# First norms of a four-FFN trunk: order of the opening loads, zero products while TensorE waits, operand parts taken from the PSUM banks

## The chip, the cores and the metric

One core of one Trainium2 chip runs the whole program. The metric is the device time of one execution in microseconds (us); for the kernel before it is the median of 3 executions. Engines are called as the profile calls them: PE (TensorE matmul), PEld (its weight load), DVE (VectorE), ACT (ScalarE), POOL (GpSimd), SP (SyncE, which here only issues DMAs). A "q" behind a name is the engine's sequencer, the place where DMAs are issued.

## The reference, cut to what matters

Two token batches, 512 and 256 rows of 1024 floats, go through the same trunk: layer 0 (a gated linear recurrence between two FFNs) and layer 1 (windowed attention between two FFNs), then a last norm. What the change touches is the very first step, the norm in front of the first FFN, and the first products of that FFN:

```python
def rmsnorm(x, g):
    xf = x.astype(F32)
    y = xf * lax.rsqrt(jnp.mean(xf * xf, axis=-1, keepdims=True) + NORM_EPS)
    return (y * g.astype(F32)).astype(x.dtype)

def swiglu_ffn(x, w1, w2):
    gate, up = jnp.split(x @ w1, 2, axis=-1)
    return (jax.nn.silu(gate) * up) @ w2

for li in range(DEPTH):
    x = x + 0.5 * swiglu_ffn(rmsnorm(x, norm_g[li, 0]), ffn_w1[li, 0], ffn_w2[li, 0])
    ...
```

All inputs are float32, `w1` is 1024 x 5632 and `w2` is 2816 x 1024 in each of the four FFNs.

## The kernel before, in words

**Tiling.** The 768 rows are six blocks of 128 rows (`x[0]` to `x[5]`), one tile of 128 x 1024 each, and two halves of three blocks. A norm (`norm_block`, L301) makes one block: ACT squares it and sums along the row (L304), ACT takes the root (L305), DVE the reciprocal (L306), and DVE multiplies the block by it (L307) into a tile `xn`. `turn` (L311) then transposes one half: for each of the eight 128-column pieces m it makes three PE transposes into one PSUM bank (L324), and ACT moves the bank out with the norm's weight as a factor (L327). `part` 0 is m = 0 to 3, `part` 1 is m = 4 to 7.

**Products.** A float32 product is made of three: every operand is split into a high part `hi` (rounded to fp32r by ACT) and a low part `lo` (DVE: value minus `hi`), and `mm3` (L260) adds hi·hi, hi·lo and lo·hi. L262, L263 and L264 are these three. For the transposed x the split is `put` and `split` (L267 on ACT, L268 on DVE), on two pieces at a time; for the weights `plain_steps` (L170 on ACT, L171 on DVE). The first two column tiles of an FFN are made in this plain form by `up_plain`, for each half of the rows a gate product (c = 0) and an up product (c = 1), each 8 pieces x 3 matmuls of 128x384. The others use a Strassen-like form with seven products, whose operands are sums and differences of the quarters of x, made by `sums`/`mix` (L351 to L355), and of w (L204, L217, POOL's `into`, L145).

**Order.** The program is traced in the order of the Python code. A planner in the compiler then orders the instructions of each engine: of those that its own cost model holds to be ready, the one traced first goes first, and a buffer must be free. `issue_after(i)` puts what is traced inside it behind `i` in the queue of `i`'s engine; it adds no wait for `i` to finish. An engine works through its queue strictly in order. `later` and `run_later` keep a list of steps that are traced at fixed places inside `up_plain` (L408) and elsewhere.

**Start.** `setup` (L92) loads the identity on SP (L101) and the norm weights as rows on ACT's queue (L109), transposes these rows on PE (L112) and copies them out on DVE (L114). `load_x` (L270) loads x[0] to x[2] on SP, then the first two weight tiles (L155), then x[3] to x[5]; norms blocks 0 to 2; turns half 0; stages (splits) the two weight tiles; and calls `load_tables` (L116), one small DMA on ACT's queue and one POOL instruction. The norms of blocks 3 to 5, the turns of half 1 and `sums` are put on the list for later. `down_quad` (L465) of the first group begins with additions in place among the six x blocks (L471, L472); their sources are ready as soon as x is loaded.

**Buffers.** PSUM has 8 banks under one tag, `big` tiles 21 slots, raw weights 4 (`wr`), split weights 8 (`w`).

## Time and profile before

| what | value |
|---|---|
| median of 3 executions | 2763.64 us (2762.39 to 2764.43) |
| profiled execution, its own time | 2764.33 us |
| span of the profiled execution, first to last instruction | 2762.5 us |
| mean granted TensorE clock over the span | 0.999 |
| PE busy | 2735.5 us in 17281 matmuls |
| DVE, ACT, POOL busy | 2102.6, 1326.6, 309.4 us |

How to read it: the profile is one execution, with the start and length of every instruction. The page gives totals; the timeline gives single instructions in order of time (start, length, engine, line, operation, tiles, count, and in brackets how long the engine sat idle before and what ended that); the windows view gives the busy time of each engine in a stretch, the granted clock (PEclk) and the DMA rate; the groups view gives sums by line and shape. Matmuls are pipelined, so the length of one is longer than the distance to the next: for throughput the distance counts.

### The profile page before, as it was taken

How to read it: one execution, taken by the hardware profiler on the slowest of the kernel's cores; microseconds unless marked ns; L12 is line 12 of the kernel's file. 1: busy time of each engine (PE TensorE's matmuls, PEld its weight loads, DVE VectorE, ACT ScalarE, POOL GpSimd, SP SyncE). 2: the span in 40 equal slices, each digit the busy share in tenths (PEclk: the TensorE clock that was granted, in tenths of full speed). 3: DMA queues.
4: the chain of work that ended last, by engine and by line, in shares of the span. 5: the costliest groups of instructions: out<-in, count | busy, mean ns of one | idle time of the engine just before them, and what ended most of it. 6: DMA issues, size and time to landing. Idle time of an engine off the chain costs nothing.

```text
span 2762.5 us, 44483 instructions
## 1 busy us (share of the span) xinstructions
PE 2735.5 (99%) x17281; PEld 2481.5 (90%) x17281; DVE 2102.6 (76%) x3662; ACT 1326.6 (48%) x2479; POOL 309.4 (11%) x315
## 2 busy tenths in 40 slices
PE   8999999999999999999999999999999999999998
PEld 8999999888888889999999999999886789999997
DVE  7888788557477568777888878887846768788877
ACT  7444444456466354443446444444546654443444
POOL 1111211000000001121111112111000001221111
PEclk9999999999999999999999999999999999999999
DMA  5544554321110324465444355544512123555443
GB/s 160 135 117 116 138 134 119 118 67 40 55 47 25 122 62 114 112 143 133 118 120 109 83 131 138 133 115 115 146 53 77 47 62 81 134 137 128 120 112 107
DMA packets 330116, 291.63 MB, mean 106 GB/s; under 512 B 11608, under 2 KB 257840, under 8 KB 329904
## 3 DMA queue, kind: packets, MB, share of 16 engines
q1 hardware_dynamic: 294064, 212.43, 25.8%
q0 software_dynamic: 31680, 62.93, 13.4%
q10 hardware_dynamic: 4160, 13.42, 1.4%
q8 instruction: 135, 2.21, 0.3%
q14 instruction: 77, 0.63, 0.1%
HBM read 216.39 MB, written 9.44 MB: 82 GB/s over the span
## 4 chain that ended last, share of the span: by engine, by line
PE 85%; DVE 10%; ACT 3%; issue 2%; DMA 0%; DVEq 0%; ACTq 0%; SPq 0%
PE ps L422 32%; PE ps L486 21%; PE ps L262 9%; PE ps L263 9%; PE ps L264 9%; DVE w L204 2%; DVE big L268 2%; PE ps L682 1%; PE ps L1218 1%; PE ps L1157 1%; PE ps L827 1%; PE ps L1209 1%; ACT w L203 1%; DVE wr L217 1%; PE ps L324 1%
## 5 line engine op out<-in xcount | busy, mean ns | idle before, releaser
L422 PE MATMUL ps<-big,w 128*128 128x384 f32 x6720 | 1174.6, 335 | 3.4 <-ACT tA L439 2.7
L422 PEld LDWEIGHTS ps<-big,w 128*128 128x128 f32 x6720 | 1165.4, 188 | 10.9 <-ACT tA L439 9.1
L203 ACT CAST w<-wr 128x512 fp32r<-128x512 f32 x600 | 415.3, 707 | 699.8 <-DVE wr L217 376.3
L204 DVE TENSOR_TENSOR w<-wr,w 128x512 fp32r<-128x512 f32 (+1 forms) x520 | 452.8, 874 | 180.1 <-ACT w L203 153.9
L486 PE MATMUL ps<-w,big 128*128 128x512 f32 x2520 | 575.9, 389 | 1.2 <-DVE x L508 1.2
L486 PEld LDWEIGHTS ps<-w,big 128*128 128x128 f32 x2520 | 472.4, 188 | 99.6 <-ACT big L267 1.6
L508 DVE SCALAR_TENSOR_TENSOR x<-ps,x 128x512 f32<-128x512 f32 x468 | 303.5, 680 | 10.5 <-PE ps L264 10.0
L145 POOL DMA_DIRECT2D s<-wr x120 | 105.0, 875 | 1667.5 <-DMA wr<-in_ffn_w_dram 784.5
L262 PE MATMUL ps<-w,big 128*128 128x512 f32 x624 | 252.5, 405 | 0.3
L264 PE MATMUL ps<-w,big 128*128 128x512 f32 x624 | 244.6, 392 | 0.9 <-DVE big L331 0.9
L263 PE MATMUL ps<-w,big 128*128 128x512 f32 x624 | 244.4, 392 | 0.0
L262 PE MATMUL ps<-big,w 128*128 128x384 f32 (+2 forms) x640 | 219.2, 344 | 2.1 <-ACT big L267 1.3
L267 ACT CAST big<-tA 128x384 fp32r<-128x384 f32 x296 | 148.0, 513 | 149.3 <-DVE tA L454 69.0
L263 PE MATMUL ps<-big,w 128*128 128x384 f32 (+2 forms) x640 | 216.4, 338 | 0.9 <-DVE big L268 0.6
L264 PE MATMUL ps<-big,w 128*128 128x384 f32 (+2 forms) x640 | 215.6, 337 | 0.0
L268 DVE TENSOR_TENSOR big<-tA,big 128x384 fp32r<-128x384 f32 x296 | 183.0, 629 | 12.7 <-ACT big L267 11.6
L171 DVE TENSOR_TENSOR w<-wr,w 128x1024 fp32r<-128x1024 f32 x92 | 111.8, 1221 | 79.0 <-ACT w L170 73.1
L262 PEld LDWEIGHTS ps<-w,big 128*128 128x128 f32 x624 | 117.2, 188 | 29.3 <-issue 6.0
L170 ACT CAST w<-wr 128x1024 fp32r<-128x1024 f32 x92 | 96.5, 1052 | 97.8 <-PE ps L263 77.8
L204 POOL TENSOR_TENSOR w<-wr,w 128x512 fp32r<-128x512 f32 x80 | 123.3, 1541 | 177.5 <-ACT w L203 156.4
L264 PEld LDWEIGHTS ps<-w,big 128*128 128x128 f32 x624 | 117.1, 188 | 27.6 <-DVE big L331 1.7
L263 PEld LDWEIGHTS ps<-w,big 128*128 128x128 f32 x624 | 117.4, 188 | 21.8 <-issue 0.4
(163 smaller groups left out, 2899.6 us busy)
## 6 DMA issues: line engine op xcount, KB each, us to landing
wr<-in_ffn_w_dram SPq DMA_DIRECT2D x264, 512.0 KB, 3.9
s<-in_ffn_w_dram SPq DMA_DIRECT2D x120, 256.0 KB, 3.3
s<-wr POOLq DMA_DIRECT2D x120, 256.0 KB, 4.5
wr<-wr POOLq DMA_DIRECT2D x80, 256.0 KB, 3.7
wr<-in_hg_w_in_dram SPq DMA_DIRECT2D x40, 512.0 KB, 3.8
wr<-wr POOLq DMA_DIRECT2D x20, 512.0 KB, 4.6
spill<-x ACTq DMA_DIRECT2D x12, 512.0 KB, 2.7
x<-spill ACTq DMA_DIRECT2D x12, 512.0 KB, 3.3
```

The costliest lines, as they stand in the source:

```text
L145: self.nc.gpsimd.dma_start(out, src, accum_op=ALU.add)
L171: self.nc.vector.tensor_sub(lo, raw, hi.bitcast(F32))
L203: nc.scalar.copy(h, src)
L204: low = (eng or nc.vector).tensor_sub(l, src, h.bitcast(F32)).ins
L262: nc.tensor.matmul(out, a[0], b[0], start=first, stop=False)
L263: nc.tensor.matmul(out, a[0], b[1], start=False, stop=False)
L264: nc.tensor.matmul(out, a[1], b[0], start=False, stop=last)
L267: self.nc.scalar.copy(hi, src)
L268: self.nc.vector.tensor_sub(lo, src, hi.bitcast(F32))
L422: self.nc.tensor.matmul(ps, a[x], b[y], start=first and k == 0 and i == 0, stop=k == 3 and i == 2, skip_group_check=True,)
L486: nc.tensor.matmul(ps, a[x], w[y], start=name == chain and kp == 0 and q == 0, stop=kp == 1 and q == 2, skip_group_check=True,)
L508: self.nc.vector.scalar_tensor_tensor(x, ps, c, x, ALU.mult, ALU.add)
```

## The change

The change rewrites the opening. The diff, cut to what the text speaks of:

```diff
+WARM = 21
...
     def setup(self, consts):
+        zero = self.tmp(TA)[:, :P]
+        nc.vector.memset(zero, 0.0)
         self.eps = cp.tile([P, 1], F32, name="eps")
         nc.vector.memset(self.eps, EPS)
+        idle = self.ps(P)
+        for _ in range(WARM):
+            nc.tensor.matmul(idle, zero, zero, start=True, stop=True)
+        raw = self.tmp(P)
+        nc.scalar.dma_start(raw, ident)
         warm = self.stat(1)
         nc.scalar.activation(warm, self.eps, AF.Sqrt)
-        raw = self.tmp(P)
-        nc.sync.dma_start(raw, ident)
...
-        pt = self.ps(n)
-        nc.tensor.transpose(pt, cols[:n, :], self.ident[:n, :n])
         self.cols = cp.tile([P, n], F32, name="cols")
-        nc.vector.tensor_copy(self.cols, pt)
+        def turn():
+            pt = self.ps(n)
+            nc.tensor.transpose(pt, cols[:n, :], self.ident[:n, :n])
+            nc.vector.tensor_copy(self.cols, pt)
+        self.turn_cols = turn
...
     def load_x(self, srcs):
...
-                order = self.norm_block(b)
-        self.turn(0, 0, 0)
-        self.turn(0, 1, 0)
+                order = self.norm_block(b, b == 1)
+        with self.tc.issue_after(self.scaled):
+            self.turn_cols()
+        self.turn(0, 0, 0, True)
         with self.tc.issue_after(order):
             self.stage_next()
             self.stage_next()
-        self.load_tables()
-        def rest():
-            for b in range(HB, NBLK):
-                self.norm_block(b)
-        self.later(rest, lambda: self.turn(1, 0, 0), lambda: self.turn(1, 1, 0), self.sums)
+        self.turn(0, 1, 0, True)
+        for b in range(HB, NBLK):
+            with self.tc.issue_after(order):
+                order = self.norm_block(b)
+        self.normed, self.mixed = order, self.scaled
+        with self.tc.issue_after(order):
+            self.load_tables()
+        self.later(lambda: None, lambda: None, lambda: self.turn(1, 0, 0), lambda: self.turn(1, 1, 0), self.sums)
 
-    def norm_block(self, b):
+    def norm_block(self, b, on_dve=False):
...
+        if on_dve:
+            nc.vector.tensor_tensor_reduce(xn, self.x[b], self.x[b], 1.0, 0.0, ALU.mult, ALU.add, r)
+        else:
+            nc.scalar.activation(xn, self.x[b], AF.Square, accum_out=r)
...
-        nc.vector.tensor_scalar(xn, self.x[b], r, None, ALU.mult)
+        self.scaled = nc.vector.tensor_scalar(xn, self.x[b], r, None, ALU.mult).ins
...
     def turn(self, half, part, row, straight=False):
...
+            if straight:
+                key = (f"b{part}{half}", m % 4 // 2)
+                if key not in self.ops:
+                    self.ops[key] = self.big([P, 2, 2, H], F32R)
+                hi, lo = (self.ops[key][:, m % 2, i, :] for i in range(2))
+            elif feeds_ffn:
                 nc.scalar.activation(self.block(part, half, m % 4), pt, AF.Copy, scale=g)
                 continue
...
             nc.scalar.activation(hi, pt, AF.Copy, scale=g)
             nc.vector.scalar_tensor_tensor(lo, pt, g, hi.bitcast(F32), ALU.mult, ALU.subtract)
...
+            if straight:
+                self.block(part, half, 0)
+                hi, lo = (self.ops[(name, kp)][:, :, i, :].bitcast(F32) for i in range(2))
+                nc.gpsimd.tensor_add(self.tn[(part, half)][:, kp], hi, lo)
+            else:
+                low = self.put(name, kp, self.tn[(part, half)][:, kp])
+                self.mixed = self.mixed and low
...
     def up_plain(self, tag, j, half):
-        self.nc.scalar.activation(t, pss[0], AF.Silu)
+        with self.tc.issue_after(self.normed) if self.normed else nullcontext():
+            self.nc.scalar.activation(t, pss[0], AF.Silu)
+        self.normed = None
...
     def down_quad(self, tag, g, hid):
-                nc.vector.tensor_add(x12, x12, x22)
-                nc.vector.tensor_sub(x21, x21, x22)
+                with self.tc.issue_after(self.mixed) if self.mixed else nullcontext():
+                    nc.vector.tensor_add(x12, x12, x22)
+                    nc.vector.tensor_sub(x21, x21, x22)
+            self.mixed = None
```

In words: the identity is loaded on ACT's queue, so that x is first on SP. PE multiplies a tile of zeros by itself 21 times before its first real work. The square of block 1 is made by DVE instead of ACT. The transposed norm weights are copied out by DVE behind the scaling of block 2. For half 0, ACT writes the high parts straight from the banks, DVE makes the low parts straight from the banks, and the sum of the two, which `sums` needs as the whole value, is made by POOL (four additions of 128x768). The norms of blocks 3 to 5 are traced in `load_x`; the first Silu, the small table of sinks, and the additions in place of the first `down_quad` are queued behind them (the additions behind the last split of half 1).

More of the change, by code (lines that the diff above doesn't have):

```diff
@@ L342, in put @@
         t = self.ops[(name, kp)] = self.big([P, 2, 2, H], F32R)
-        self.split(src, t[:, :, 0, :], t[:, :, 1, :])
+        return self.split(src, t[:, :, 0, :], t[:, :, 1, :])
     def operand(self, name, k):
```

15 lines of the change are left out of this document (7 added, 8 removed).

## Prediction

> **What bounds the kernel now.** I read the page's totals and the chain that ended last first, then the windows view of the opening.
>
> ```profile
> PE 2735.5 (99%) x17281; PEld 2481.5 (90%) x17281; DVE 2102.6 (76%) x3662; ACT 1326.6 (48%) x2479; POOL 309.4 (11%) x315
> PE 85%; DVE 10%; ACT 3%; issue 2%; DMA 0%; DVEq 0%; ACTq 0%; SPq 0%
> 30.00:60.00 30.00, 30.00 (x178) 29.97 (x177) 27.90 (x37) 20.44 (x35) 3.65 (x3) 1.00 0.30 80
> 13.64:17.05 3.41, 1.71 (x8) 1.46 (x9) 2.47 (x4) 3.41 (x7) 0.00 (x0) 1.00 1.09 338
> 17.05:20.47 3.42, 3.27 (x11) 2.77 (x10) 3.10 (x5) 3.42 (x5) 0.00 (x0) 0.50 1.17 290
> ```
>
> PE carries the span; 27 of 2762.5 us are free of it. From 30 us on it never pauses for 30 us (third row), so a gain of the opening is kept if nothing else becomes late, and it cannot exceed what PE loses before 30 us. The last two rows (after the window: PE, PEld, DVE, ACT, POOL busy, then granted clock) show one of these losses: 3.41 us at half clock, behind a stretch of the same length in which PE was half busy. The others stand in the timeline:
>
> ```profile
> 0.74 0.39 SPq L101 DMA_DIRECT2D tB<-in_ident_dram  x1
> 1.18 1.37 SPq L278 DMA_DIRECT2D x<-in_x_prompt_dram  x3
> 5.58 1.06 ACT L304 ACTIVATE big<-x 128x1024 f32<-128x1024 f32 x1 [2.89 <-DMA x<-in_x_prompt_dram]
> 7.23 0.38 PE L112 MATMUL ps<-ident_r,tB 88*128 88x88 f32 x1 [7.23 <-DMA tB<-in_hg_g_norm_dram]
> 6.96 1.04 ACT L304 ACTIVATE big<-x 128x1024 f32<-128x1024 f32 x1
> 8.33 1.04 ACT L304 ACTIVATE big<-x 128x1024 f32<-128x1024 f32 x1
> 10.02 0.75 DVE L307 TENSOR_SCALAR big<-x,stat 128x1024 f32<-128x1024 f32 x1
> 10.07 1.05 ACT L170 CAST w<-wr 128x1024 fp32r<-128x1024 f32 x1 [0.28 <-DMA wr<-in_ffn_w_dram]
> 11.16 1.22 DVE L171 TENSOR_TENSOR w<-wr,w 128x1024 fp32r<-128x1024 f32 x1 [0.38 <-ACT w L170]
> 8.09 5.38 PE L324 MATMUL ps<-ident_r,big 128*128 128x128 f32 x24 [0.48 <-DVE big L307]
> 25.39 1.03 PE L324 MATMUL ps<-ident_r,big 128*128 128x128 f32 x8
> 12.02 2.00 ACT L327 ACTIVATE big<-ps,cols 128x384 f32<-128x384 f32 x4 [0.90 <-PE ps L324]
> 14.79 0.44 PE L262 MATMUL ps<-big,w 128*128 128x384 f32 x1 [1.31 <-ACT big L267]
> 16.24 0.35 PE L262 MATMUL ps<-big,w 128*128 128x384 f32 x1
> 16.60 0.34 PE L264 MATMUL ps<-big,w 128*128 128x384 f32 x1
> 17.50 0.52 PE L262 MATMUL ps<-big,w 128*128 128x384 f32 x1
> 17.82 0.52 PE L263 MATMUL ps<-big,w 128*128 128x384 f32 x1
> 21.57 0.33 PE L264 MATMUL ps<-big,w 128*128 128x384 f32 x1
> 25.21 0.34 PE L264 MATMUL ps<-big,w 128*128 128x384 f32 x1
> 27.65 0.44 PE L262 MATMUL ps<-big,w 128*128 128x384 f32 x1 [0.70 <-ACT w L170]
> 29.95 0.34 PE L262 MATMUL ps<-big,w 128*128 128x384 f32 x1
> ```
>
> The 24 transposes stood 0.22 us apart ((5.38 − 0.4) / 23), the eight at 25.39 0.11: although the windows show 1.00 there, PE ran at half clock before 13.64. Block 2's scaling ends at 10.77, but the transposes, slow as they are, release the first bank only at 12.02; then come the move out of the bank, the split on ACT, and the first product at 14.79. The first plain product (24 matmuls) ends with the one at 21.57; at full clock matmuls stand 0.173 us apart (21 of them from 21.57 to 25.21), at half clock 0.32 (17.50, 17.82). I measure at 29.95, when before has done 51 product matmuls and 24 + 16 transposes. 27 matmuls and 16 transposes lie behind 21.75: 27 × 0.173 + 16 × 0.108 = 6.4 us of 8.2; 1.8 are lost, partly because the third weight's split waits on ACT (27.65).
>
> **The change part by part.** *Loads.* The identity leaves SP, so x is issued at 0.74 instead of 1.18; I move every landing of x and w 0.44 us forward. In ACT's queue the identity takes the head place of the sinks' table, of like length. x[0] is then there at 5.14, x[1] by 6.5, x[2] by 7.9 (ACT starts on them in the rows, less 0.44; they may land earlier), the first weight at 9.63.
>
> *Square of block 1 on DVE.* Nearest rows, and those for the new low parts and the zeros:
>
> ```profile
> L1173 DVE CUSTOM_DVE_ANT_0 big<-ps,big,nsinks 128x256 f32<-128x256 f32 x64 | 27.3, 478 | 3.4 <-PE ps L1157 3.4
> L1173 DVE CUSTOM_DVE_ANT_0 big<-ps,big,nsinks 128x384 f32<-128x384 f32 x32 | 17.8, 610 | 1.2 <-PE ps L1157 1.0 <-PE ps L264 0.2
> 512.22 1.66 DVE L331 SCALAR_TENSOR_TENSOR big<-ps,cols,big 128x384 fp32r<-128x384 f32 x3
> 609.81 1.95 PE L803 MATMUL ps<-x,big 128*128 128x128 f32 x16
> 48.40 1.91 POOL L204 TENSOR_TENSOR w<-wr,w 128x512 fp32r<-128x512 f32 x1 [10.95 <-ACT w L203]
> 49.07 1.78 DVE L204 TENSOR_TENSOR w<-wr,w 128x512 fp32r<-128x512 f32 x1
> 283.56 1.87 DVE L508 SCALAR_TENSOR_TENSOR x<-ps,x 128x512 f32<-128x512 f32 x3
> 283.83 1.29 POOL L204 TENSOR_TENSOR w<-wr,w 128x512 fp32r<-128x512 f32 x1 [1.42 <-ACT w L203]
> ```
>
> 132 ns per 128 columns makes 1.27 us for 1024, with the accumulator's read about 1.35 against ACT's 1.04 and its read. It runs 6.5 to 7.85; ACT's root of block 1 waits for it, and block 2's square is queued behind that root: 8.15. From there as before (8.33 to 10.77, 2.44 us): block 2 is scaled at 10.6, against 10.77. So the norms gain only 0.2 us. If the planner puts block 0's reciprocal and scaling (0.75 for the scaling, about 0.95 together) ahead of the square, the square starts at 7.6 and the end is 11.7, a loss of 0.9; put behind it, block 0 is ready for PE at 8.8 instead of 8.09.
>
> *Zeros.* They begin near 1.1, when DVE has cleared the tile. A float32 product of this size takes 0.112 us ((1.95 − 0.27) / 15), 0.22 at half clock: 21 × 0.22 = 4.7, until 5.8. PE's next work, the transpose of the norm weights, waited for its DMA until 7.23, so even 6 us of zeros would cost nothing. Do they buy the clock? Between 5.8 and 8.85 PE has one transpose to do, and the row 13.64:17.05 shows that half a stretch of work was not enough to keep it. I take no gain: the 24 transposes begin at 8.85, end at 14.2, and the full clock comes, as before, from their own 5.4 us of work. [...]
>
> *Straight parts.* Gone from the path: one of two ACT passes. With transposes at half clock the first bank is ready at 12.7, its high part at 13.3. DVE, which has made the first weight's low part by 12.1 (from 10.84, a quarter us for the copy of the norm weights, plus 1.22) and can make the second's by 13.3, then makes eight low parts at 0.53 each ((1.66 − 0.61) / 2): 13.3 + 8 × 0.53 = 17.5; ACT keeps pace (0.5 each, 12.02's row). PE needs 0.52 per piece, so the first product ends two matmuls behind the last low part: 17.9 instead of 21.75.
>
> *POOL's four sums* are new: 128x512 took 1.3 to 1.9 us there, so 1.5 times that, 1.9 to 2.9 each. They are not on PE's path, but DVE's op with two SBUF inputs at 49.07 took 1.78 beside POOL (two of that shape take 1.28 at 16.51, below), while three with a bank as input (283.56) were not slowed. The low parts read a bank and are safe; a weight's low part or a scaling that falls beside POOL's work pays up to 1.9. I add 0.5 for this and the order on DVE together (bounds 0 and 3.0): the second product starts to run freely at S = 18.4.
>
> *Norms 3 to 5 earlier, Silu behind them.* The three blocks need ACT for 3 × 1.4 us behind the eight moves out of the banks, to about 21 or 22, and their DVE work. Silu's table load now stands between the roots of these blocks, and each switch costs 1.28; two of three go:
>
> ```profile
> 23.27 1.28 ACT L413 ACT_TABLE_LOAD   x1
> 16.51 1.28 DVE L472 TENSOR_TENSOR x<-x,x 128x512 f32<-128x512 f32 x2
> 37.00:60.00 23.00, 23.00 (x135) 23.00 (x134) 22.67 (x31) 13.46 (x24) 2.35 (x2) 1.00 0.20 53
> ```
>
> So ACT reaches the third weight at about 22 to 23, and PE wants it at 18.4 + 4.2 = 22.6; I leave 0.6 us of wait (bounds 0 and 1.5). Behind the waiting Silu are only later casts. The sinks' table waits on POOL for its DMA behind the roots; POOL's next work there feeds products after 55 us. The six additions (0.65 each, two in 1.28) leave DVE's early time and come back behind half 1's splits, where DVE is full until 60 (last row); they are due only at the first down product, beyond 80 us, so I count nothing.
>
> *Sum.* 18.4 + 6.4 + 0.6 = 25.4 where before stands at 29.95: 4.5 us less. The profiled execution, 2764.33 us (span 2762.5 and 1.8 around it), becomes 2759.8; it is 0.7 above the median of 2763.64, so the median becomes 2759.1. Between S = 17.2 without wait and S = 20.4 with 1.5 it is 2757.3 to 2762.0.
>
> **The rivals.** *The zeros hold the clock.* The wake-up comes around 5 us, the pause to 8.85 doesn't lose it, and transposes follow the norms at full pace: first bank at 10.9, DVE's low parts from 12.06 to 16.3, the second weight's behind them (17.5), S = 17.2. That is 23.6 without wait, or 2757.3; with 0.3 of wait 2757.6. For it: zeros fill more than a 3.41 us stretch; against: the half-busy row. [...]
>
> *The clock comes late.* The clock changed at 13.64, 17.05 and 20.47, in steps of 3.41 us that follow no instruction; here they may lie otherwise, and the full clock come a step later. At half clock 16 of the first 24 products at 0.32 from 14.2 to 19.3 and 8 at 0.173 give S = 20.7: 2.3 us less gain, 2761.4.
>
> *VectorE's order.* Square behind block 0's scaling (1.1), second weight's low part beside POOL (1.9): S = 20.9, 2761.6. For it: the planner goes by its own costs; against: the low parts have other work to fill the time.
>
> *VectorE falls behind*, the one that ends slower. If all four POOL sums (4 × 2.3) hold DVE, and the square and the dearer low parts add 1.9, DVE has 11.1 more to do before 37 us; it had 6.2 us idle from 13 to 37, so it enters the full stretch 4.9 late, if the six additions that left are replaced by six that come ahead of the first pair's weights. There the margin was 4.4 (first low part done at 50.85, 49.07's row; first use at 55.3):
>
> ```profile
> 13.00:25.00 12.00, 9.99 (x46) 8.83 (x45) 9.55 (x14) 11.97 (x22) 1.03 (x1) 0.86 1.00 283
> 25.00:37.00 12.00, 10.86 (x70) 10.11 (x69) 8.27 (x12) 11.60 (x19) 2.16 (x3) 1.00 0.62 143
> L422 PE MATMUL ps<-big,w x168: 334/334/444, 55.3 to 84.9; 128*128 128x384 f32 x168
> ```
>
> With PE 4.5 earlier it would wait 5.0: 2764.1, slower by 0.5. It decides from 4.4 us of lateness; against it, the planner ranks those additions behind the pairs.
>
> **How the numbers follow.** Forecast 0.50, zeros hold 0.20, late clock 0.16, VectorE's order 0.10, VectorE behind 0.04. 0.2% is 5.5 us, about what a measurement of this kernel can tell from no change: faster by more needs less than 2758.1, which the first rival gives nearly always and the forecast's lower end sometimes: 0.22. Slower by more, above 2769.2, only if the last goes far beyond its price: 0.02. The rest, 0.76. Range: 2757.2 to 2762.1, from the first rival to the forecast's upper end, which holds the middle two.
>
> **What would show it.** First product matmul near 13.5 to 14.5 instead of 14.79, the 24th near 17.9, PE without a wait on L170 near 22 to 23; transposes 0.22 us apart (forecast) or 0.11 (first rival); DVE ops of 1.8 us and more beside POOL's sums; a single Silu table load before 40 us. I am wrong if PE waits for DVE between 30 and 85 us, if the weights land later than 9.6, or if the gain at 30 us is no longer there at the end.

## The result and the profile after

| what | before | after |
|---|---|---|
| median | 2764.49 us (22 executions, 2762.39 to 2767.02) | 2760.18 us (22 executions, 2758.40 to 2761.64) |
| ratio of the times | | 0.9982, 95% interval 0.9977 to 0.9988 |
| span of the profiled execution | 2762.5 us | 2758.4 us |

The change is worth 4.3 us, 0.18%; 2759.1 with 2757.2 to 2762.1 was forecast. Many lines have new numbers in the kernel after: the transposes of x are now L339, the moves out of the banks L351 (high) and L352 (low), POOL's sums L358, a weight's cast and low part L180 and L181, the plain products L272 to L274, the products of the pairs L452 (L422 before), the down product L518 (L486), its additions to x L540 (L508), half 1's sums and differences L378 (L351 before), a quad weight's cast and low part L213 and L214 (L203, L204).

First the opening, in the timeline of the kernel after (start, length, engine, line, operation, count, idle time and what ended it):

```profile
1.06 7.47 PE L103 MATMUL ps<-tA 128*128 128x128 f32 x42 [1.06 <-DVE eps L100]
8.44 3.09 PE L339 MATMUL ps<-ident_r,big 128*128 128x128 f32 x24
10.59 2.00 ACT L351 ACTIVATE big<-ps,cols 128x384 fp32r<-128x384 f32 x4
12.39 0.44 PE L272 MATMUL ps<-big,w 128*128 128x384 f32 x1 [0.86 <-DVE big L352]
12.95 9.23 POOL L358 TENSOR_TENSOR big<-big 128x768 f32<-128x768 f32 x4 [12.50 <-DVE big L352]
13.83 2.05 DVE L181 TENSOR_TENSOR w<-wr,w 128x1024 fp32r<-128x1024 f32 x1
15.93 0.44 PE L274 MATMUL ps<-big,w 128*128 128x384 f32 x1 [0.66 <-DVE w L181]
17.60 0.51 PE L272 MATMUL ps<-big,w 128*128 128x384 f32 x2
18.06 2.41 DVE L181 TENSOR_TENSOR w<-wr,w 128x1024 fp32r<-128x1024 f32 x1
20.58 2.15 DVE L322 TENSOR_SCALAR big<-x,stat 128x1024 f32<-128x1024 f32 x1
21.86 1.28 ACT L442 ACT_TABLE_LOAD   x1
```

The zeros are 42 matmuls and reach to 8.52. The transposes behind them stand 0.12 us apart in the mean ((3.09 − 0.27) / 23), not 0.22: the pace of full clock (0.11 for the eight at 25.39 in before) from the first of them on (the zeros themselves went from 0.213 to 0.112 us apart at 6.36). The first product matmul stands at 12.39 (14.79 before); the one at 17.60 opens the second product (21.75 before). Three operations of DVE that lie beside POOL's sums take 2.05, 2.41 and 2.15 us; one of the first kind takes 1.21 to 1.23 alone, the scaling 0.75. Silu's table is loaded once before 40 us, as forecast (before: at 23.27 and, after a load for the roots at 25.07, again at 36.12).

Then the stretch to the first down product. For each line the view of one source line gives first and last start (the last two numbers before the semicolon); first before, then after:

```profile
L351 DVE TENSOR_TENSOR big<-big,big x2: 951/952/952, 37.2 to 38.0; 128x768 f32<-128x768 f32 x2
L508 DVE SCALAR_TENSOR_TENSOR x<-ps,x x3: 681/684/685, 87.9 to 90.1; 128x512 f32<-128x512 f32 x3
```

```profile
L378 DVE TENSOR_TENSOR big<-big,big x2: 952/953/954, 34.3 to 35.2; 128x768 f32<-128x768 f32 x2
L452 PE MATMUL ps<-big,w x168: 334/334/334, 50.7 to 79.6; 128*128 128x384 f32 x168
L540 DVE SCALAR_TENSOR_TENSOR x<-ps,x x6: 682/684/685, 85.8 to 94.3; 128x512 f32<-128x512 f32 x6
```

The products of the pairs run from 50.7 to 79.6, where before had 55.3 to 84.9 (shown in the prediction): 4.6 us ahead, then 5.3, because before's wait for ACT among them is gone. But DVE begins half 1's sums only 2.9 us earlier and makes the first addition behind the down product only 2.1 earlier. In the view of PE's waits (waiting line, releaser, us, times, longest) the difference appears as a wait that before did not have (first view, after). Before has one at a later down product that after does not have (second view):

```profile
PE ps L518 <- DVE x L540: 2.0, 1, 2.0
```

```profile
PE ps L486 <- DVE x L508: 1.2, 1, 1.2
```

Behind the wait PE needs a little time to get back into step: of 5.3 us, 3.0 are left once the first down product runs again (matmul against matmul of the two timelines), and 4.1 at the end (2762.5 − 2758.4). On the way about 1.5 come back at 1255 us, where before has the wait of the second view, and almost one more in small waits of the later groups (see "between, p5 on DVE"); a stretch of half clock at 2078 us in the profile after takes about 1.1 again (4.9 ahead before it, 3.8 behind it). There is one profile of before, and whether each execution of it waits at 1255 us is not known.

### The profile page after: what moved, and what is told of

Same layout as the page of the kernel before. It is cut to its first block, busy times and chain, and to the rows that moved or that the text cites. A ratio compares the mean times of both kernels' runs of the same rounds, so it can differ in the third digit from the quotient of the medians.

```text
span 2758.4 us, 44576 instructions
## 1 busy us (share of the span) xinstructions
PE 2739.3 (99%) x17323; PEld 2486.0 (90%) x17323; DVE 2100.0 (76%) x3669; ACT 1321.8 (48%) x2471; POOL 322.6 (12%) x319
## 4 chain that ended last, share of the span: by engine, by line
PE 86%; DVE 9%; ACT 2%; issue 2%; DMA 1%; SPq 0%; DVEq 0%; ACTq 0%; POOLq 0%
PE ps L452 33%; PE ps L518 21%; PE ps L272 9%; PE ps L274 9%; PE ps L273 9%; DVE w L214 2%; DVE big L278 2%; PE ps L714 1%; PE ps L1250 1%; PE ps L1189 1%; PE ps L859 1%; PE ps L1241 1%; DVE wr L227 1%; ACT w L213 1%; PE ps L339 1%
## 5 line engine op out<-in xcount | busy, mean ns | idle before, releaser
L452 PE MATMUL ps<-big,w 128*128 128x384 f32 x6720 | 1174.3, 334 | 2.1 <-ACT tA L469 1.4
L452 PEld LDWEIGHTS ps<-big,w 128*128 128x128 f32 x6720 | 1165.3, 188 | 9.4 <-ACT tA L469 7.8
L213 ACT CAST w<-wr 128x512 fp32r<-128x512 f32 x600 | 415.9, 706 | 692.9 <-DVE wr L227 342.6
L214 DVE TENSOR_TENSOR w<-wr,w 128x512 fp32r<-128x512 f32 (+1 forms) x520 | 448.5, 866 | 182.1 <-ACT w L213 162.9
L518 PE MATMUL ps<-w,big 128*128 128x512 f32 x2520 | 575.7, 389 | 2.0 <-DVE x L540 2.0
L518 PEld LDWEIGHTS ps<-w,big 128*128 128x128 f32 x2520 | 472.6, 188 | 100.1 <-DVE x L540 2.7
L540 DVE SCALAR_TENSOR_TENSOR x<-ps,x 128x512 f32<-128x512 f32 x468 | 304.0, 683 | 10.4 <-PE ps L274 10.0
L272 PE MATMUL ps<-w,big 128*128 128x512 f32 x624 | 252.5, 405 | 0.3
L274 PE MATMUL ps<-w,big 128*128 128x512 f32 x624 | 244.6, 392 | 1.0 <-DVE big L352 1.0
L272 PE MATMUL ps<-big,w 128*128 128x384 f32 (+2 forms) x640 | 218.2, 343 | 0.9 <-DVE big L352 0.9
L274 PE MATMUL ps<-big,w 128*128 128x384 f32 (+2 forms) x640 | 215.0, 336 | 0.7 <-DVE w L181 0.7
L278 DVE TENSOR_TENSOR big<-tA,big 128x384 fp32r<-128x384 f32 x296 | 181.4, 623 | 13.2 <-ACT big L277 12.2
L181 DVE TENSOR_TENSOR w<-wr,w 128x1024 fp32r<-128x1024 f32 x92 | 114.0, 1244 | 78.0 <-ACT w L180 72.0
L214 POOL TENSOR_TENSOR w<-wr,w 128x512 fp32r<-128x512 f32 x80 | 127.2, 1590 | 176.2 <-ACT w L213 154.8
L272 PEld LDWEIGHTS ps<-w,big 128*128 128x128 f32 x624 | 117.2, 188 | 29.4 <-issue 6.0
L180 ACT CAST w<-wr 128x1024 fp32r<-128x1024 f32 x92 | 96.5, 1052 | 97.3 <-PE ps L273 77.7
L274 PEld LDWEIGHTS ps<-w,big 128*128 128x128 f32 x624 | 117.1, 188 | 27.6 <-DVE big L352 1.7
L155 POOL DMA_DIRECT2D wr<-wr x100 | 87.5, 875 | 441.3 <-ACT w L213 176.2
```

The source lines that it names most:

```text
L155: self.nc.gpsimd.dma_start(out, src, accum_op=ALU.add)
L181: self.nc.vector.tensor_sub(lo, raw, hi.bitcast(F32))
L213: nc.scalar.copy(h, src)
L214: low = (eng or nc.vector).tensor_sub(l, src, h.bitcast(F32)).ins
L272: nc.tensor.matmul(out, a[0], b[0], start=first, stop=False)
L274: nc.tensor.matmul(out, a[1], b[0], start=False, stop=last)
```

## The experiments

Each kernel differs from the changed one by the edit shown (one from the kernel before). All were timed in turn with the kernel before, in three sets that each used one chip: 2764.61, 2764.74 and 2763.57 us was the median of before there. Theories by letter: **A**, the zeros carry the opening's gain; **B**, POOL's sums take part of it back because they hold DVE; **C**, the late additions cause the wait at 86 us; **D** and **E** came up between the sets. The intervals of the times are 3 to 7 us wide, so the times alone tell only the two kernels with p5 on DVE from the changed one; the others are told apart by places in their profiles, one execution each. The table gathers what the profiles gave: starts from the rows of single lines, the wait of the first down product from the view of waits, and whether the windows view shows a stretch of 3.41 us at half clock right behind it.

| kernel | half 1's sums | pairs' products | first addition | PE's wait there | half clock | median us | ratio (95%) |
|---|---|---|---|---|---|---|---|
| before | 37.2 | 55.3 | 87.9 | none | no | 2764.49 | |
| after | 34.3 | 50.7 | 85.8 | 2.0 | no | 2760.18 | 0.9982 (0.9977 to 0.9988) |
| after, again | 33.9 | 50.3 | 85.4 | 2.0 | yes | 2759.86 | 0.9983 (0.9975 to 0.9992) |
| no zeros | 34.3 | 50.7 | 85.7 | 1.9 | yes | 2761.73 | 0.9992 (0.9983 to 1.0000) |
| zeros alone | 36.2 | 54.2 | 86.8 | none | no | 2761.01 | 0.9990 (0.9981 to 0.9999) |
| additions free | 36.9 | 51.8 | 87.5 | 2.3 | yes | 2763.51 | 0.9996 (0.9987 to 1.0005) |
| sums late on POOL | 36.9 | 51.0 | 87.8 | 2.3 | no | 2762.86 | 0.9995 (0.9986 to 1.0004) |
| additions between | 35.2 | 50.4 | 85.9 | 2.5 | yes | 2760.31 | 0.9986 (0.9977 to 0.9995) |
| sums on DVE | 35.0 | 48.7 | 84.3 | 1.8 | no | 2758.37 | 0.9976 (0.9967 to 0.9985) |
| between, p5 on DVE | 35.2 | 50.4 | 84.7 | 0.9 | no | 2752.28 | 0.9955 (0.9943 to 0.9968) |
| not straight | 34.5 | 50.0 | 85.4 | 1.7 | no | 2760.75 | 0.9989 (0.9980 to 0.9998) |
| half the zeros | 34.4 | 50.7 | 85.8 | 2.0 | yes | 2760.34 | 0.9988 (0.9979 to 0.9997) |
| moves first | 31.2 | 48.3 | 83.2 | 2.3 | yes | 2758.59 | 0.9981 (0.9972 to 0.9989) |
| moves first, p5 on DVE | 31.1 | 48.1 | 82.4 | 0.9 | no | 2748.61 | 0.9948 (0.9935 to 0.9960) |

**No zeros.** Theory A.

```diff
-        zero = self.tmp(TA)[:, :P]
-        nc.vector.memset(zero, 0.0)
...
-        idle = self.ps(P)
-        for _ in range(WARM):
-            nc.tensor.matmul(idle, zero, zero, start=True, stop=True)
```

> The changed kernel without its zero products (no zero tile, no zero matmuls, nothing else changed). Theory A (the zeros, which run on until 8.52 us, hold the full clock through transposes and first products): transposes 0.21 to 0.22 us apart from about 8.4, ending near 13.8 instead of 11.5; first bank ready near 12.3 instead of 10.6; first products partly at half clock; at 60 us PE is 2.1 to 3.1 us ahead of the kernel before instead of 4.6, and the whole gain is 1.5 to 3.0 us instead of 4.3. Rival (the transposes wake the clock by themselves and VectorE's low parts cover the rest, as the prediction had it): at 60 us PE is still 4.0 us or more ahead, and the time is within 0.5 us of the changed kernel's.

The timeline of this kernel at the transposes:

```profile
8.20 4.79 PE L334 MATMUL ps<-ident_r,big 128*128 128x128 f32 x24 [0.43 <-DVE big L317]
11.06 2.00 ACT L346 ACTIVATE big<-ps,cols 128x384 fp32r<-128x384 f32 x4 [0.81 <-PE ps L334]
12.74 0.42 PE L267 MATMUL ps<-big,w 128*128 128x384 f32 x1
13.00 0.33 PE L268 MATMUL ps<-big,w 128*128 128x384 f32 x1
```

4.79 us for 24 instead of 3.09, 0.20 us apart in the mean ((4.79 − 0.27) / 23; 0.22 in before), and yet the first bank is moved at 11.06 (10.59 with zeros) and the first product stands at 12.74 (12.39). In before the 17th transpose releases the first bank; in this kernel it is the 12th (10.61), so that bank's three transposes lie earlier in PE's order. At the pairs both stand at 50.7. A's number for the pairs fell: with everything else in place the zeros buy nothing there. Whether they would without POOL's holds was not tried. The time is 2.9 us below before, 4.3 in the other set for the kernel with zeros. That alone would fit A (1.5 to 3.0), but the intervals overlap, and this profile has the stretch of half clock behind the wait.

**Zeros alone**, in the kernel before:

```diff
+        zero = self.tmp(TA)[:, :P]
+        nc.vector.memset(zero, 0.0)
         self.eps = cp.tile([P, 1], F32, name="eps")
         nc.vector.memset(self.eps, EPS)
+        idle = self.ps(P)
+        for _ in range(WARM):
+            nc.tensor.matmul(idle, zero, zero, start=True, stop=True)
```

> The kernel before with the 21 zero products put in front and nothing else. Theory A: transposes 0.11 apart, first product at 13.6 to 14.0 instead of 14.79, no half clock between 17 and 20.5; at 60 us PE is 1.0 to 2.5 us ahead of the kernel before, and so is the whole time. Rival (order and straight parts make the gain, the clock none of it): within 0.5 us of the kernel before.

1.1 us ahead at the pairs (54.2 against 55.3): with before's order of work the full clock (matmuls 0.17 us apart from 15.52 on, where before has 0.32 from 17.50 to 18.46) is worth that much in the opening, and the first product comes at 14.25, later than A's 13.6 to 14.0. But the time is 3.6 us below before, more than A's 1.0 to 2.5, with an interval from 0.3 to 5.3. In the profile the lead stays at 1.1 to 1.5 until 1200 us, is 2.8 at about 1340, because this execution has no wait at 1255 us either, and 3.6 at the end. So a part of what either kernel gains at the end is not made in the opening, and by their times alone the zeros could not be told from the whole change.

**Additions free**, theory C: the six additions may fall where the planner likes.

```diff
-                with self.tc.issue_after(self.mixed) if self.mixed else nullcontext():
-                    nc.vector.tensor_add(x12, x12, x22)
-                    nc.vector.tensor_sub(x21, x21, x22)
+                nc.vector.tensor_add(x12, x12, x22)
+                nc.vector.tensor_sub(x21, x21, x22)
```

> The changed kernel with the six additions of the first down product free again in VectorE's queue (not behind half 1's splits). Rival C: they leave the stretch from 54 to 75 us, the wait in front of the first down product shrinks by 1.3 to 2.0 us, and the gain is 5.3 to 6.3 us. Theory B: that wait changes by less than 0.7 us, or the additions, back between 13 and 31 us, cost as much in front, so that the time stays within 0.8 us of the changed kernel's.

They came at 17.60, beside POOL's sums, the first two in 4.30 us instead of 1.28; half 1's sums began 2.6 us later than in the changed kernel and the wait grew to 2.3. C fell. The time is 1.1 us below before, not within B's 0.8 of the changed kernel's gain; half clock follows the wait here. To queue them late is right, but not because of the wait at 86.

**Sums late on POOL**, theory B: the four sums behind POOL's first weight work, beyond 24 us.

```diff
...
-                nc.gpsimd.tensor_add(self.tn[(part, half)][:, kp], hi, lo)
+                self.whole.append((self.tn[(part, half)][:, kp], hi, lo))
...
+        with self.tc.issue_after(self.last_into):
+            for t, hi, lo in self.whole:
+                nc.gpsimd.tensor_add(t, hi, lo)
```

> The changed kernel with POOL's four sums traced at the end of the opening and queued on POOL behind the accumulating DMAs of the first weight pair, so that they fall after about 25 us instead of 13 to 22. Theory B (POOL's sums hold VectorE's two-input operations for 3.4 us between 13.8 and 22.7, which makes norms 3 to 5, half 1 and the operand sums late, and so the weights of the first down product): weight low parts take 1.2 us instead of 2.0 to 2.4, PE's waits at 15.9 and 24.8 shrink, the operand sums start 1.5 to 3 us earlier, PE's wait in front of the first down product (2.0 us at 86.6) falls below 0.5, and the whole gain is 5.5 to 7.0 us. Rival C (the six additions on VectorE at 54 to 75 us make that wait): it stays at 1.5 us or more and the gain is at most 5.0 us.

Up to 24 us no operation of DVE is held, and the second product begins at 16.54 instead of 17.60. Then the sums hold others; the timeline:

```profile
24.59 2.14 POOL L311 TENSOR_TENSOR big<-big 128x768 f32<-128x768 f32 x1
26.99 6.05 POOL L311 TENSOR_TENSOR big<-big 128x768 f32<-128x768 f32 x3
27.32 6.14 DVE L278 TENSOR_TENSOR big<-tA,big 128x384 fp32r<-128x384 f32 x1 [3.95 <-ACT big L277]
34.39 0.44 PE L273 MATMUL ps<-big,w 128*128 128x384 f32 x1 [1.95 <-DVE big L278]
```

A split of 128x384, 0.55 us where it is not held, takes 6.14, until POOL's three additions (26.99 to 33.04) are through. That POOL's sums hold DVE, as B has it, is seen here too; B's time was wrong (1.8 us below before, 5.5 to 7.0 forecast), because the hold moved and did not go.

**Theory D** after these: from half 1's sums on DVE is the bound until the first down product, so its load counts there.

**The changed kernel again**:

> The changed kernel as it stands, beside the variants of it on one chip. Theory D (from half 1's splits on, VectorE sets the time of the first down product, so of the 4.6 us won in the opening only what VectorE itself wins is kept): the profile again shows PE 4.4 to 4.8 us ahead of the kernel before between 36 and 74 us, a wait of 1.8 to 2.2 us on L540 near 86, and 2.8 to 3.2 us ahead at 90; time 2.5 to 4.5 us below before. Rival (what is lost at 86 us is an event of the one execution that was profiled): no wait of more than 0.5 us at 86, 4.3 us or more ahead at 90, and the shorter time comes with it.

The wait is there again, 2.0 us, and so is the shorter time: 4.9 us below before, a little more than D's 4.5. PE is 5.0 us ahead at the pairs (4.4 to 4.8 forecast). What differs between the two executions is the clock: half clock follows the wait here, so 1.8 are left behind it instead of D's 2.8 to 3.2 (the last section shows it).

**Additions between**: behind block 5's scaling, where DVE had idle time.

```diff
-                low = self.put(name, kp, self.tn[(part, half)][:, kp])
-                self.mixed = self.mixed and low
+                self.put(name, kp, self.tn[(part, half)][:, kp])
```

> One line less: the six additions of the first down product are queued behind the scaling of block 5 instead of behind half 1's last split, so they can fall where VectorE stands idle (some 4 us between 25.6 and 34 in the changed kernel) instead of among the pairs (54 to 75). They cost 6 x 0.65 = 3.9 us. Theory D: half 1's sums begin not later than 35.5, VectorE has 3.9 us less to do before the first down product, the wait on L540 near 86 shrinks to below 0.5, PE is 4.2 us or more ahead of the kernel before at 90 us, and the time is 1.5 to 2 us below that of the changed kernel on the same chip. Rival (the wait at 86 comes from the weights, not from VectorE's load: raw buffers, DMA and the casts of the down weights): the wait stays within 0.4 of its size and the time equals the changed kernel's within 0.7. Second rival: the idle stretches cannot be filled, because the additions stand ahead of the norms' and half 1's work in a strict queue: half 1's sums begin 2 us or more later and PE waits before 60.

D failed as it was put: 3.9 us less for DVE to do before the down product, and the wait is 2.5. The time is 0.5 us above the changed kernel's on the same chip, as its first rival had it (within 0.7), though the wait grew by 0.5, a little beyond that rival's 0.4. Half 1's sums began 0.9 later than in the first profile after, and the stretch from there to the first addition shrank by 0.8 only. Why it did not shrink by the work taken out of it shows in what DVE waits for at its end. The timeline of the kernel after:

```profile
65.43 0.68 DVE L227 TENSOR_TENSOR wr<-wr,wr 128x512 f32<-128x512 f32 x1
66.24 19.12 SPq L165 DMA_DIRECT2D wr<-in_ffn_w_dram  x3
74.43 0.86 POOL L155 DMA_DIRECT2D wr<-wr  x1 [9.04 <-DMA wr<-in_ffn_w_dram]
79.07 2.00 ACT L213 CAST w<-wr 128x1024 fp32r<-128x1024 f32 x2 [6.57 <-DMA wr<-wr]
80.15 1.23 DVE L214 TENSOR_TENSOR w<-wr,w 128x1024 fp32r<-128x1024 f32 x1 [4.21 <-ACT w L213]
85.82 0.68 DVE L540 SCALAR_TENSOR_TENSOR x<-ps,x 128x512 f32<-128x512 f32 x1
86.56 0.73 PE L518 MATMUL ps<-w,big 128*128 128x512 f32 x2 [2.01 <-DVE x L540]
```

Read from the bottom: PE needs a bank, which L540 frees; L540 stands in DVE's queue behind the low part of a down weight (80.15), for which DVE sat idle 4.21 us; that waits for ACT's cast, this for a DMA that POOL issued at 74.43 to add one weight quarter to another, this for the load that SP could issue at 66.24, when DVE's sum at 65.43 had freed raw buffers. From that sum to L540 are 20.4 us of loads, a DMA that adds, casts and DVE's queue; ahead of it lie 31.1 us of DVE work from the start of half 1's sums (34.3). Before has the same two stretches, 30.5 and 20.2 (37.2, 67.6, 87.9).

**Sums on DVE**, behind block 5's scaling, and none on POOL.

```diff
...
-                nc.gpsimd.tensor_add(self.tn[(part, half)][:, kp], hi, lo)
+                self.whole.append((self.tn[(part, half)][:, kp], hi, lo))
...
+        with self.tc.issue_after(self.scaled):
+            for t, hi, lo in self.whole:
+                nc.vector.tensor_add(t, hi, lo)
```

> The four whole-value sums of half 0 are made by VectorE behind the scaling of block 5 instead of by GpSimd. Theory D (VectorE's load counts): they cost 4 x 0.97 = 3.9 us, fill the idle stretches between 25 and 34, no operation of VectorE is held before 40 us; PE is 5.5 to 6.5 us ahead at 36, as where the sums come late, and what is ahead at 90 us is 2.5 to 4.0, because the load on VectorE is what it was. Rival (GpSimd's holds, 3.4 us of them, are what sets VectorE back): 5 us or more ahead at 90 and a time 2 us below the changed kernel's.

Nothing is held in the opening; PE is 6.5 us ahead at the pairs, and with the pairs' products ending at 78.1 (84.9 before) and a wait of 1.8 there are 4.8 left behind the wait. That is more than D's 2.5 to 4.0 and just short of the rival's 5; the time is 1.5 us below the changed kernel's on the same chip, a little less than the rival's 2. DVE's own sums delay half 1's to 35.0, but from there it is only 49.2 to the first addition.

**Between, p5 on DVE**: as "additions between", and the low part of every pair's p5 weight moves from POOL to DVE.

```diff
-            low = split(name, own[name], nc.gpsimd if up and name == "p5" else None)
+            low = split(name, own[name])
```

> The additions as in the kernel with them in the idle stretch, and besides it the low part of p5 of every up pair made by VectorE (0.65 us each) instead of GpSimd (1.9 to 3.8 us each, holding operations of VectorE with two SBUF inputs). Theory D by load alone: two such parts fall before 85 us, 1.3 us more for VectorE against holds of about that size, so PE stands at 90 us within 0.7 of the kernel without this edit, and the whole time within 1. Rival (the holds are the larger cost, in every pair): 1 us or more better at 90, and 2 us or more in the whole time.

8.0 us less than "additions between" on the same chip: the rival, by far. The groups view (busy us, mean ns, idle), first without and then with this edit:

```profile
L214 POOL TENSOR_TENSOR w<-wr,w 128x512 fp32r<-128x512 f32 x80 | 128.9, 1612 | 173.2 <-ACT w L213 151.6 <-DMA s<-in_ffn_w_dram 21.6
L214 DVE TENSOR_TENSOR w<-wr,w 128x512 fp32r<-128x512 f32 (+1 forms) x520 | 452.7, 874 | 185.5 <-ACT w L213 168.2 <-issue 12.3 <-PE ps L451 1.6
L278 DVE TENSOR_TENSOR big<-tA,big 128x384 fp32r<-128x384 f32 x296 | 181.6, 624 | 12.7 <-ACT big L277 11.6
```

```profile
L214 DVE TENSOR_TENSOR w<-wr,w 128x512 fp32r<-128x512 f32 x600 | 473.7, 794 | 236.5 <-ACT w L213 213.6 <-PE ps L451 17.4
L278 DVE TENSOR_TENSOR big<-tA,big 128x384 fp32r<-128x384 f32 x296 | 160.0, 552 | 6.0 <-ACT big L277 5.6
```

80 parts more on DVE cost 21.0 us (473.7 − 452.7), not 80 x 0.68 = 54 (0.68 is one part alone, in the timeline), and the splits of L278 lose 21.6 (181.6 − 160.0): the two together stay the same and 129 us of POOL are free. The gain grows all through the FFN stages, in steps. The view of waits leaves out what is below 0.15 us, but the timeline shows one step; without the edit:

```profile
237.80 1.64 POOL L214 TENSOR_TENSOR w<-wr,w 128x512 fp32r<-128x512 f32 x1
237.95 2.85 DVE L278 TENSOR_TENSOR big<-tA,big 128x384 fp32r<-128x384 f32 x3 [0.58 <-ACT big L277]
247.80 0.53 ACT L489 ACTIVATE tA<-tA 128x384 f32<-128x384 f32 x1 [0.61 <-DVE tA L488]
248.23 0.46 ACT L468 COPY tA<-ps 128x384 f32<-128x384 f32 x1
248.75 0.62 PE L451 MATMUL ps<-big,w 128*128 128x384 f32 x2 [0.15 <-ACT tA L468]
```

and the same three splits with it:

```profile
234.09 1.50 DVE L278 TENSOR_TENSOR big<-tA,big 128x384 fp32r<-128x384 f32 x3
```

Beside POOL's low part the splits take 1.35 us more. DVE's chain behind them ends late, the Silu (L489) waits for it, and ACT's copy of a bank (L468), queued behind the Silu, frees that bank late; PE's matmul at 248.75 comes 0.49 us behind the one before instead of 0.17. This happens once ahead of each of the 16 down products that aren't an FFN's first, for 5.7 us in all (with the slower step behind each; 7.3 in before, 6.4 in the kernel after). With the edit there is one such wait, of 1.0 us, near the end. The two profiles differ by 10.2 us: besides these waits, 3.6 lie ahead of 95 us, where the wait is shorter and no half clock follows it, and about 1.2 in a stretch of half clock at 2080 us that only the kernel without the edit has.

**Theory E**, from these profiles: the first addition comes 49 to 51.5 us after DVE begins half 1's sums.

**Not straight**: half 0 by the old path of two ACT passes, no sums on POOL.

```diff
-        self.turn(0, 0, 0, True)
+        self.turn(0, 0, 0)
...
-        self.turn(0, 1, 0, True)
+        self.turn(0, 1, 0)
```

> The changed kernel without the straight parts: half 0's banks are moved out by ACT, then split by ACT and VectorE as before; no sums on GpSimd. Theory E (from 34 us on the end of the first down product hangs on when VectorE can begin half 1's sums: over eight kernels the first L540-type addition came 49.2 to 51.5 us after it): ACT has 3.4 us more ahead of blocks 3 to 5, half 1's sums begin at 35.5 to 36.8 instead of 33.9, the first 24 products end near 20.5, PE is 1.5 to 2.5 us ahead of the kernel before at 36 us and 0.8 to 1.8 at 90; the time is 1.5 to 3 us above the changed kernel's. Rival (the zeros and the earlier norms carry the gain, ACT's second pass hides): 3.5 us or more ahead at 36 and at 90.

The forecast failed and its rival was right: the second product begins 0.5 us later than with straight parts (18.14 against 17.60), but nothing holds DVE, and at the pairs this kernel is 0.7 us ahead of the changed one (50.0 against 50.7); 3.6 are left behind the wait. In the profile the straight parts and the sums that they need cancel. The time, 2.8 us below before, doesn't decide it: in the other sets the changed kernel is 4.3 and 4.9 below, which fits the forecast of 1.5 to 3 us more as well, and the intervals overlap.

**Half the zeros**:

```diff
-WARM = 21
+WARM = 11
```

> 11 zero products instead of 21: 22 matmuls of 0.213 us, until about 5.8, which is what the prediction took 21 to be. Theory (the clock is set anew every 3.41 us by how busy PE was in the stretch that ends): the stretch with the pause from 5.8 to 8.4 is less than half busy, so a stretch of half clock falls into the transposes, the first product comes 0.2 to 0.5 us later than 12.4, and 0.5 us at most of it is left at 36 us; time within 1 us of the changed kernel's. [...]

The windows view of this kernel (stretch; busy us of PE, PEld, DVE, ACT, POOL; granted clock; DMA):

```profile
2.12:5.54 3.42, 3.42 (x18) 3.42 (x18) 0.23 (x1) 1.43 (x3) 0.00 (x0) 1.00 0.96 362
5.54:8.95 3.41, 1.36 (x11) 1.05 (x10) 2.81 (x6) 2.14 (x7) 0.00 (x0) 1.00 1.05 321
8.95:12.36 3.41, 3.41 (x19) 3.30 (x18) 3.03 (x7) 2.36 (x5) 0.00 (x0) 0.50 1.09 373
```

As the theory had it: the stretch with the pause is 1.36 busy of 3.41, and the next one is at half clock (granted 0.50). The first eight transposes still stand 0.11 us apart. The first product comes at 12.49 instead of 12.39, less late than the forecast's 0.2 to 0.5, and at the pairs nothing of it is left (50.7). The time is 3.2 us below before, in another set than the changed kernel's 4.3 and 4.9.

**Moves first**: the sums on DVE, and ACT moves half 1's banks ahead of the second Silu and of the first hidden units' splits, for which it sat idle 3.66 us.

```diff
...
-        with self.tc.issue_after(self.normed) if self.normed else nullcontext():
+        first = self.normed or (self.opening and half == 0 and self.moved0)
+        with self.tc.issue_after(first) if first else nullcontext():
             self.nc.scalar.activation(t, pss[0], AF.Silu)
...
+                    if self.opening and half == 0:
+                        with self.tc.issue_after(self.moved):
+                            for j in range(PLAIN):
+                                put(f"b{j}0", ts[2 * j], 0)
```

> VectorE makes half 0's four sums behind block 5's scaling (as in the run with the sums there), and ACT moves half 1's banks out ahead of the second Silu and of the splits of the first hidden units, which stood in front of them and waited (3.7 us of ACT idle). Theory E: half 1's sums begin at 30.5 to 32 instead of 33.9 (changed kernel) or 35.0 (sums on VectorE alone), the first L540-type addition comes at 80 to 82.5, PE's wait there falls below 0.5, PE is 6 us or more ahead of the kernel before at 36 and at 90 us, and the time is 1.5 to 2.5 us below that with the sums on VectorE alone, 6.5 to 8.5 below before. Rival (the chain of the down product's weights does not follow the start of the sums): the addition stays at 84 to 85.5, the wait at 1.8 or more, and the time at 2758 to 2760.

Half of E: the sums begin at 31.2 as forecast, PE is 7.0 us ahead at the pairs; but the first addition comes 52.0 behind, at 83.2, 0.7 later than the latest forecast, PE waits 2.3, and half clock follows. The time, 5.0 us below before, is the rival's (2758 to 2760), not E's 6.5 to 8.5. The windows at that place:

```profile
81.37:84.79 3.42, 1.13 (x6) 0.71 (x5) 3.42 (x6) 1.87 (x4) 0.00 (x0) 1.00 0.34 102
84.79:88.20 3.41, 3.41 (x10) 2.64 (x9) 3.41 (x8) 1.57 (x4) 0.00 (x0) 0.50 0.19 57
```

What brought DVE forward here (3.2 us at half 1's sums, 2.7 at the first addition, against the kernel after) brought PE forward too (2.4 at the pairs), and the wait stays.

**Moves first, p5 on DVE**:

> The same with the low part of p5 on VectorE besides (8 us in the run that had it). If the two gains are of different places, as theory E has it (the one before 90 us, the other in all later stages), they add up: 2747 to 2750, 15 to 17 us below before. Rival (both take away the same waits): 2751 or more.

The two add up: 2748.61 us, 15 below before and the fastest kernel of the study. Of its 15 us, 10.0 are the gain over "moves first" in the same set, somewhat more than the 8.0 that p5 gave above. The wait is 0.9, as in the other kernel with p5 on DVE, and none of the small waits at the later groups is left.

## Why the prediction was right, and where it was not

The time, the sum (4.5 us; 4.6 at the pairs, 4.3 in the medians) and the range held, but several of the steps behind the sum did not, and their errors cancelled. That is luck in part. The second product began 0.8 us earlier than forecast (17.60 for 18.4), while the transposes of half 1 waited 0.9 us for DVE's scaling, where 0.6 had been left for ACT's split of the third weight. And that the end agrees with the opening is luck as well: the loss at the first down product, the wait gone at 1255 us, the smaller waits in the groups and the half clock at 2078 us are in no term of the sum, and they nearly cancel.

*Loads and norms* went as worked out: the square of block 0 and all behind it came somewhat earlier (4.86 for 5.14), block 2 was scaled at 10.16 instead of 10.6, and DVE's square stayed within its price (1.23 for 1.35).

*Zeros.* "21 × 0.22 = 4.7, until 5.8" was mis-sized by two: the 21 products stand in the trace as 42 matmuls, 7.47 us. There was no pause of 3 us behind them, the clock stayed, and the transposes went at 0.12 instead of 0.22. That is the outcome of the rival that the zeros hold the clock, but not by its mechanism: it had the clock outlast the pause, and here there was none. With half the zeros, the count that the prediction had meant, the pause came and the clock was lost behind it, as the prediction said, though only from 8.95 to 12.36 (granted 0.50). "I take no gain" was right for the pairs: without zeros they stand at the same 50.7. The first product, forecast for 13.5 to 14.5, came at 12.39, and at 12.74 without zeros; so 0.35 of this is the clock, and most is the first bank, which the prediction had ready at 12.7 at half clock. It let the transposes begin at 8.85 and counted 17 to the first bank, the order of before; without zeros they begin at 8.20, and the 12th releases the bank, so that ACT moves it at 11.06. As forecast, full clock came behind transposes alone: without zeros these 24 were all that PE did from 8.2 to 12.7, and the product at 13.00 took 0.33 us, the length at full clock (0.52 at half clock, in the prediction's row at 17.50).

*Straight parts.* Forecast: the first product ends at 17.9 instead of 21.75; measured 17.6, where the second begins. But the kernel with the old path has that at 18.1. So straight parts and POOL's sums together are worth 0.5 us there, and the straight parts without the sums on POOL 1.6 (16.5 with the sums on DVE). The rest of the 4 us isn't the clock either, where the rest of the change is in place: without zeros it is 17.6 as well. What is left are the norms in order, the earlier first bank, the loads and the square, and how it divides among them stays open, because they were not tried alone. The additions taken out of DVE's early time count only further on: 1.1 us at the pairs by the run with free additions, nothing at the second product (17.3 there).

*POOL's sums.* 0.5 us was too little: without them the second product begins 1.1 us earlier (16.50 with the sums on DVE), the pairs 2.0. The three held operations of the first profile stand for 3.4 us (0.83, 1.19 and 1.40 over their unheld lengths). A longer case is the split in "sums late on POOL", 6.14 us instead of 0.55 beside three additions of POOL. The low parts with a bank as input were as safe as forecast: four beside the sums (L352 at 15.80) took 2.18 us together, the four that began ahead of them (11.72) 2.19.

*The step that failed* is the one about what is due "only at the first down product, beyond 80 us, so I count nothing", and the margin of the rival "VectorE falls behind". That margin, 4.4 us, was taken at the first pair's weights; the tight place was the end of the chain, the first down product, where before had only 1.2: PE came 5.3 us earlier there, DVE only 2.1, and PE waits 2.0 (5.3 − 2.1 − 2.0 = 1.2). The prediction named PE waiting for DVE between 30 and 85 us as what would make it wrong; the wait ended at 86.56, having begun at 84.5, and so lay across that bound. That the six additions would be its cause, as the rival had it, did not hold: with them elsewhere the wait was 2.5 and 2.3.

## What to carry to other kernels

A lead that one engine wins in the opening lasts only as far as the tightest margin behind it: look for that at each later place where another engine's chain (here buffer release, load, accumulate, cast, split) meets the first one, not only at the next. In these runs DVE's operations with SBUF operands alone took longer beside POOL's elementwise ones (2.05 us for 1.22 and 2.15 for 0.75 in the kernel after, 6.14 for 0.55 with the sums late), so work given to POOL to spare DVE may cost DVE as much: 80 parts moved back left DVE's busy time in L214 and L278 where it was (634.3 us without, 633.7 with) and gained 8 us. And a change of the opening is judged at the end as well: the lead here went 4.6, 5.3, 3.0, 4.9, 3.8 and 4.1 us on its way.

## What the runs showed of the hardware

**Half clock came in stretches of 3.41 us.** In the profile of before the granted clock falls to 0.50 at 17.05 us, is back at 1.00 at 20.47 and falls again at 2757.95; in that of after the same happens at 2078.25, 2081.66 and 2754.09. The long distances, 2737.48 and 672.43 us, are 802.1 and 197.0 times 3.413. The place differs from profile to profile: at the first down product the stretch at 0.50 begins at 84.79 ("moves first"), 86.57 (after, again), 87.11 ("additions between"), 87.31 (no zeros) and 87.46 (half the zeros), 3.41 us at 0.50 in each. Stretches of 3.41 us just ahead of one at half clock had, by the windows view, this much PE work: 0.96 us in "additions between" (from 83.69), 1.13 in "moves first" (81.37), 1.36 and 1.40 with half the zeros (5.54 and 84.04), 1.41 in after, again (83.15), 1.48 without zeros (83.90), 1.71 in before (13.64) and 1.76 in after (2074.83). Others were followed by full clock: 1.68 without straight parts (83.85), 1.73 in after (84.86) and 2.11 in before (2081.58). Between 1.68 and 1.76 it thus went both ways; the modelled ends of matmuls blur the sum. On the way up, in before's opening (where the view shows 1.00 up to 17.05): behind 2.51 us of PE work (6.81 to 10.22) the transposes still stood 0.21 us apart, and behind 3.25 (10.22 to 13.64) products stood 0.18 apart (16.24, 16.43, 16.60). The two executions of the changed kernel had one and the same wait of 2.0 us, and half clock behind it in one of them. The windows of the first, then of the second:

```profile
81.45:84.86 3.41, 3.09 (x14) 2.23 (x12) 3.38 (x6) 0.99 (x2) 0.00 (x0) 1.00 0.00 0
84.86:88.28 3.42, 1.73 (x8) 1.43 (x9) 3.42 (x8) 1.70 (x4) 0.00 (x0) 1.00 0.52 152
88.28:91.69 3.41, 3.41 (x17) 2.83 (x16) 3.41 (x8) 1.91 (x4) 0.00 (x0) 1.00 0.00 1
```

```profile
83.15:86.57 3.42, 1.41 (x7) 0.86 (x6) 3.42 (x7) 1.87 (x5) 0.00 (x0) 1.00 0.17 50
86.57:89.98 3.41, 3.41 (x10) 2.63 (x9) 3.41 (x8) 1.78 (x4) 0.00 (x0) 0.50 0.35 103
```

10 matmuls instead of 17 in the stretch: a wait of 2.0 us takes 2.3 or 3.9 us of the lead over before (5.3 to 3.0, 5.7 to 1.8). The first execution's wait (84.5 to 86.56) lies across two stretches with 3.09 and 1.73 us of PE work, the second's (84.15 to 86.16) inside one with 1.41. A wait of 2.0 us was therefore not safe here.

**POOL's operations took longer as well.** One low part of 128x512 on POOL, 1.91 us in before (48.40), took 7.50 with the additions between (45.59) and 10.79 with the sums on DVE (41.66), while DVE worked beside it.
